# Splitting every other prompt weight with rounding and accumulating transfers issued from POOL, one conditioning part per sequence, and trigonometric tables stored in two parts

## The chip, the cores and the metric

The kernel runs on one core of one Trainium2 chip. The metric is the device time of one execution in microseconds (us), the median of several runs. Engines are named as in the profile: PE (matrix multiplications; PEld are its weight loads), DVE (vector), ACT (activations and copies), POOL (small scalar work before the change), SP (issues the DMAs).

## The reference

One layer of an encoder is applied to two sequences that share all weights: a prompt of 512 rows ("p") and a sample of 1024 rows ("s"), each 1024 wide, in float32.

```
h = rms_norm(x, g_pre_mix) * (1 + sc1) + sh1          # sh, sc, gt from silu(c) @ w_ada, six parts
xa, ya, xb, ga, gb = split(h @ w_in)
xa = depthwise_conv(xa)                                # 4 taps
h_lru = rg_lru(xa, forward) + rg_lru(xa, backward)     # two gates by head, then a scan over time
y_a = (h_lru * gelu(ya)) @ w_a_out
y_b = real(fft2(xb by group)) @ w_b_out
x = x + gt1 * rms_norm((sigmoid(ga) * y_a + sigmoid(gb) * y_b) @ w_o, g_post_mix)
h = rms_norm(x, g_pre_ffn) * (1 + sc2) + sh2
val, gate = split(depthwise_conv(h @ w_up))            # 3 taps
x = x + gt2 * rms_norm((gelu(gate) * val) @ w_down, g_post_ffn)
```

The conditioning vector c differs by sequence, so each of the six parts (shift, scale and gate, for two sub-layers) is needed once for p and once for s. The gates gt1 and gt2 are the third part of each.

## The kernel before, in words

**Products in three passes.** A float32 operand is held as a rounded high part and a remainder (hi, lo), and a product is the sum of three matmuls: hi by hi, hi by lo, lo by hi. For a weight the order inside each block of 128 rows is w.hi with x.hi, w.hi with x.lo, w.lo with x.hi (`passes`, L206, `fm_mm`, L209), so the lo part of a weight is first wanted at the third matmul of its unit.

**Units.** A weight tile of 128x1024 (512 KB) is a unit. `load_unit` (L122) has SP fetch it into one of three `raw` buffers; `prep_unit` (L126) splits it into one of four `hl` buffers: the high part is a copy on ACT (L109, where `on_act` is set) or on DVE (L111), the low part a subtraction on DVE (L112). A prompt unit is 24 matmuls of 512 columns.

**Order.** `emit` (L170) walks a list of steps written by hand. Before the matmuls of unit i it prepares the unit i+3 and issues loads up to three units beyond that; a unit's `hl` buffer is the one that the fourth unit before it leaves. All engines run their instructions in the order of the program, and so does SP with its DMA issues: one that waits for a free `raw` buffer holds up those behind it. `defer` puts the second half of an operation some steps later.

**The prompt's mixer.** After a lead-in come, in this order: projections (ga, xa, gb, two units to a group, f = 0 and f = 1) with four RG-LRU units woven in (`lru_step`, L666), the forward transform of the folded Fourier input (`pq_steps`, L821, whose inputs are fetched back from DRAM as `hr` and paired up on DVE and ACT), four groups of the gelu gate (`ya_steps`, L769), two units of trigonometric tables (`dft_steps`, L884), and `merge_steps` (L936): four groups g, each of two units of w_a (24 matmuls each) and two short units of w_b (13 matmuls of 258 columns each, prepared on DVE alone). For g = 0 the w_a units come first, for the others the w_b units. Into the merge the rows of the sample's first norm are woven: for each of 8 tiles a square with its sum on ACT (L413), two instructions on POOL (L430, L431), and one step later the scaling on ACT (L418).

**An RG-LRU unit** has 24 matmuls into four PSUM buffers. ACT follows with eight tanh (L684), four exp (L692), four tanh (L694) and two relu (L696) in the same step, and one step later, behind a table load, two square roots (L710). DVE multiplies, scans and adds (L703 to L723).

**Conditioning.** `ada_steps(2)` computes the gate part gt1 with eight weight tiles from DRAM and, for each of them, a product with a running sum on DVE for p and one for s (L337): 16 steps placed among the prompt's ya units. `gate_rows` (L363) transposes the result and stores it to DRAM, from where `gate_steps` (L372) broadcasts the rows.

**The sample's mixer** repeats this with one unit to a group and 48 matmuls to a projection unit. Feed-forward parts follow.

Of the kernel before, what the change touches and what calls it, by code (L numbers as in the profile page):

```python
# [18 lines left out]
KT = D // 128  # L19
# [42 lines left out]
class Unit:  # L62
    def __init__(self, src, cols, mix=False, on_act=False, whole=True):
        self.src, self.cols, self.mix, self.on_act, self.whole = src, cols, mix, on_act, whole
        self.raw = self.hi = self.lo = None
# [7 lines left out]
class Enc:  # L73
# [47 lines left out]

    def load_unit(self, u):  # L122
        u.raw = self.sb.tile([128, u.cols], F32, tag="raw", bufs=RAW_BUFS, name=self.nm("raw"))
        self.nc.sync.dma_start(out=u.raw, in_=u.src)

    def prep_unit(self, u):  # L126
        hl = self.sb.tile([128, 2, u.cols], F32R, tag="hl", bufs=HL_BUFS, name=self.nm("hl"))
        u.hi, u.lo = hl[:, 0, :], hl[:, 1, :]
        src = u.raw
        if u.mix:  # L130
            nc = self.nc
            src = self.big([128, u.cols], name="wb")
# [20 lines left out]
    def load_to(self, k):  # L153
        while self.ld < min(len(self.units), k):
            if self.units[self.ld].unit is not None:
                self.load_unit(self.units[self.ld].unit)
            self.ld += 1

    def prep_to(self, k):
        while self.pp < min(len(self.units), k):  # L160
            self.load_to(self.pp + 1)
            u = self.units[self.pp]
            if u.pre is not None:
                u.pre()
# [67 lines left out]

    def fm_steps(self, sq, table, tiles, xh, xl, post, on_act=False):
        box = {}
        steps = []
        for f, m in enumerate(tiles):
            u = Unit(table[m], KT * 128, on_act=on_act)

# [82 lines left out]

    def ada_steps(self, job):

# [9 lines left out]
        def dot(k, s):  # L333
            def f():
                w = box.pop(k) if s else box[k]
                out = w if s else self.big([128, 1024], name="adap")
                nc.vector.scalar_tensor_tensor(  # L337
                    out=out, in0=w, scalar=0.5, in1=self.cvec[s], op0=ALU.mult, op1=ALU.mult,
                    accum_out=self.mod[:, job, s, k:k + 1])
            return f  # L340

        def out():
            bias = self.vec[:, V_BADA + job * 8:V_BADA + job * 8 + 8]
            sub, kind = divmod(job, 3)
            for s in range(2):
                m = self.mod[:, job, s, :]
                nc.vector.tensor_tensor(out=m, in0=m, in1=bias, op=ALU.add)
            for s in range(2):
                m = self.mod[:, job, s, :]
# [4 lines left out]
                if kind == 2:  # L354
                    g = self.vec[:, (V_GOM, V_GOF)[sub]:(V_GOM, V_GOF)[sub] + 8]
                    nc.vector.tensor_tensor(out=self.gtg[:, sub, s, :], in0=m, in1=g, op=ALU.mult)
        steps = [Step(loads=[] if s else [ld(k)], post=dot(k, s)) for k in range(8) for s in range(2)]
        steps += [Step(post=out)]
        if job % 3 == 2:
            steps += [Step(), Step(), Step(), Step(mm=lambda: self.gate_rows(job // 3))]  # L360
        return steps

    def gate_rows(self, sub):  # L363
        nc = self.nc
        ps = self.ps([16, 128])
        self.trans(ps, self.gtg[:, sub].rearrange("p s k -> p (s k)"), self.ident)
        sb = self.sb.tile([16, 128], F32, tag="gaterow", bufs=1, name=self.nm("gr"))
        nc.vector.tensor_copy(sb, ps)
        self.grow[sub] = self.dram([16, 128], f"grow{sub}")
        self.defer(lambda: nc.sync.dma_start(out=self.grow[sub], in_=sb), 1)  # L370

    def gate_steps(self, sq, sub, box):  # L372
        def ld():
            box["gate"] = self.big([128, 1024], name="gate")
            src = self.grow[sub].rearrange("(s k) c -> s (k c)", s=2)[sq.idx:sq.idx + 1, :]
            self.nc.sync.dma_start(out=box["gate"], in_=src.to_broadcast([128, 1024]))
# [289 lines left out]
    def lru_step(self, sq, g, box, hs):  # L666
        nc = self.nc
        n, nf = sq.n, sq.nf
        cols = nf * 512
        u = Unit(self.a["w_lru_" + sq.name][g], cols)  # L670
        th = {}
# [69 lines left out]
    def mix_heads(self, sq, hb, hs, sig, lead=0):  # L741
# [6 lines left out]
        def proj(nm, g, post):  # L748
            return self.fm_steps(sq, self.a[nm], tiles(g), xh, xl, post, on_act=True)

# [18 lines left out]
    def ya_steps(self, sq, hb, hs, yb):  # L769
# [15 lines left out]
        for g in range(sq.groups):  # L785
            tiles = range(g * sq.nf, (g + 1) * sq.nf)
            steps += self.fm_steps(sq, self.a["w_ya"], tiles, lambda: hb["hi"], lambda: hb["lo"],
                                   lambda ps, g=g: post(ps, g), on_act=True)
        steps[-1].post, last = None, steps[-1].post
# [94 lines left out]
    def dft_steps(self, sq, pq, z):  # L884
# [51 lines left out]
    def merge_steps(self, sq, yb, z, sig, mg):  # L936
# [5 lines left out]
        for g in range(sq.groups):  # L942
# [62 lines left out]
            for f in range(nf):  # L1005
# [3 lines left out]
            as_ = self.fm_steps(sq, self.a["w_a"], range(g * nf, (g + 1) * nf),  # L1009
                                lambda: yb["hi"], lambda: yb["lo"], post_a, on_act=True)  # L1010
            first, second = (as_, bs) if g == 0 else (bs, as_)
# [392 lines left out]
def encoder(ctx: ExitStack, tc: tile.TileContext, a, outs):  # L1404
# [6 lines left out]
    with tc.manual_schedule():  # L1411
# [24 lines left out]
        steps = place(steps, side, [ya - 10] + [ya - 4 + i for i in range(16)] + [ya + 13] + [ya + 22] * 9)  # L1436
# [26 lines left out]
def _dft(n):  # L1463
# [6 lines left out]
    for fn in (np.cos, np.sin):  # L1470
# [4 lines left out]
        w = (w * (0.5 / math.sqrt(n))).reshape(rows // 128, 128, nch, HALF).transpose(2, 1, 0, 3)  # L1475
        out.append(np.ascontiguousarray(w.astype(np.float32)).reshape(nch, 128, rows // 128 * HALF))
    return out


# [90 lines left out]
```

## Time and profile before

| | |
|---|---|
| median of 3 runs | 2103.14 us (2102.98 to 2104.68) |
| the profiled execution's own time | 2103.23 us |
| its span, first to last instruction | 2101.1 us |
| around the span | 2.1 us |
| busy in the span: PE, PEld, DVE, ACT, POOL | 98%, 80%, 68%, 45%, 3% |
| granted TensorE clock, mean | 0.997 of full speed |
| DMA traffic | 284.57 MB, all issued by SP |

Busy time of PE says little by itself, since matmuls are pipelined and a matmul that waits for the next weight still counts. The idle time of PEld, the weight loads, shows where PE had to wait for an operand.

### The profile page before, as it was taken

To read this page: it belongs to the slowest core of one execution; us is meant where nothing else is said; L and a number is where in the kernel's file an instruction comes from. 1 tells how busy PE (TensorE), PEld (TensorE's weight loads), DVE (VectorE), ACT (ScalarE), POOL (GpSimd) and SP (SyncE) were. 2 spreads that over 40 slices of the span, in tenths; PEclk is the share of its full clock that TensorE was granted. 3 is DMA by queue.
4 is the path that set the end of the run, shared out by engine and by line. 5 is a ranking of instruction groups with operands and counts; after the bars stand their busy time and mean duration, and the time that the engine had idled before them with its cause. 6 is when DMAs were issued, how large, how long until landed. Compare 5 with 4: busy or idle time off the path is not lost.

```text
span 2101.1 us, 24339 instructions
## 1 busy us (share of the span) xinstructions
PE 2068.3 (98%) x9602; PEld 1687.5 (80%) x9602; DVE 1420.8 (68%) x1798; ACT 944.8 (45%) x1213; POOL 55.3 (3%) x132
## 2 busy tenths in 40 slices
PE   7999999999999999999999999999999999999998
PEld 6777778888888888888888888888888888888887
DVE  4677888677667664656576445749687887875553
ACT  2377555355565632135333336633344444454442
POOL 0000010000000000000100001000000000000000
PEclk9999999999999999999999999999999999999999
DMA  9643475632233314343543324332122222284422
GB/s 342 206 131 130 145 259 188 236 135 96 100 105 99 112 50 145 121 146 122 217 147 116 111 96 166 100 123 88 61 76 83 83 81 81 100 313 165 143 92 109
DMA packets 91121, 284.57 MB, mean 135 GB/s; under 512 B 9056, under 2 KB 20736, under 8 KB 91008
## 3 DMA queue, kind: packets, MB, share of 16 engines
q1 hardware_dynamic: 91008, 283.03, 39.3%
q8 instruction: 75, 1.23, 0.2%
q14 instruction: 38, 0.31, 0.0%
HBM read 237.87 MB, written 45.12 MB: 135 GB/s over the span
## 4 chain that ended last, share of the span: by engine, by line
PE 87%; DVE 5%; ACT 4%; issue 2%; DMA 2%; POOL 0%; SPq 0%; DVEq 0%; POOLq 0%; ACTq 0%
PE ps L201 86%; PE ps L204 1%; DVE hl L112 1%; ACT th L684 1%; ACT th L694 1%; DVE xc L658 1%; ACT ea L692 1%; DMA hr<-hrowp 1%; ACT xn L413 0%; DVE th L715 0%; DVE th L720 0%; DVE th L718 0%; DMA x<-in_x_sample_dram 0%; DMA x<-in_x_prompt_dram 0%; ACT hl L109 0%
## 5 line engine op out<-in xcount | busy, mean ns | idle before, releaser
L201 PE MATMUL ps<-hh,hl 128*128 128x512 f32 x2144 | 632.6, 394 | 3.5 <-DVE hl L112 3.0
L201 PEld LDWEIGHTS ps<-hh,hl 128*128 128x128 f32 x2144 | 402.2, 188 | 99.5 <-DVE hl L112 4.3
L201 PE MATMUL ps<-hl,ah 128*128 128x512 f32 x1440 | 452.3, 395 | 0.0
L112 DVE TENSOR_TENSOR hl<-raw,hl 128x1024 fp32r<-128x1024 f32 (+2 forms) x240 | 286.8, 1200 | 172.3 <-ACT hl L109 170.8
L201 PE MATMUL ps<-hl,hl 128*128 128x512 f32 x1072 | 380.8, 394 | 0.0
L201 PE MATMUL ps<-hx,wq 128*128 128x512 f32 x1596 | 370.9, 394 | 0.0
L109 ACT ACTIVATE hl<-raw 128x1024 fp32r<-128x1024 f32 (+1 forms) x222 | 232.5, 1053 | 279.3 <-PE ps L201 235.2
L201 PEld LDWEIGHTS ps<-hx,wq 128*128 128x128 f32 x1596 | 299.7, 188 | 71.0 <-DVE wq L1251 0.2
L201 PEld LDWEIGHTS ps<-hl,ah 128*128 128x128 f32 x1440 | 269.0, 188 | 61.8
L201 PE MATMUL ps<-hl,al 128*128 128x512 f32 x720 | 283.9, 394 | 0.0
L201 PEld LDWEIGHTS ps<-hl,hl 128*128 128x128 f32 x1072 | 201.4, 188 | 47.6
L201 PEld LDWEIGHTS ps<-hl,al 128*128 128x128 f32 x720 | 135.2, 188 | 32.0
L1347 DVE SCALAR_TENSOR_TENSOR cf<-ps,vec,cf 128x511 f32<-128x511 f32 (+1 forms) x100 | 75.3, 808 | 83.7 <-ACT cf L1339 83.5
L201 PE MATMUL ps<-yh,hl 128*128 128x512 f32 x384 | 111.8, 394 | 0.6 <-DVE yb L991 0.3
L1250 ACT ACTIVATE wq<-wsum 128x512 fp32r<-128x512 f32 x76 | 46.1, 629 | 118.0 <-DVE wsum L1261 118.0
L1195 DVE SCALAR_TENSOR_TENSOR cf<-cq,vec,cf 128x1023 f32<-128x1023 f32 x76 | 97.1, 1277 | 0.0
L1339 ACT ACTIVATE cf<-ps,vec 128x512 f32<-128x512 f32 (+1 forms) x50 | 39.1, 827 | 105.8 <-PE ps L201 105.8
L201 PEld LDWEIGHTS ps<-yh,hl 128*128 128x128 f32 x384 | 71.5, 188 | 17.6 <-DVE yb L991 0.8
L112 DVE TENSOR_TENSOR al<-fq,ah 128x512 fp32r<-128x512 f32 x88 | 57.2, 686 | 32.3 <-PE ps L201 18.4
L201 PE MATMUL ps<-hx,hl 128*128 128x512 f32 x288 | 66.9, 394 | 0.0
L201 PE MATMUL ps<-yl,hl 128*128 128x512 f32 x192 | 65.3, 394 | 0.0
L658 DVE SCALAR_TENSOR_TENSOR xc<-ps,vec,xc 128x511 f32<-128x511 f32 (+3 forms) x48 | 46.9, 1012 | 25.7 <-ACT xc L650 25.1
(182 smaller groups left out, 2325.0 us busy)
## 6 DMA issues: line engine op xcount, KB each, us to landing
raw<-in_w_up_dram SPq DMA_DIRECT2D x88, 512.0 KB, 3.5
raw<-in_w_down_dram SPq DMA_DIRECT2D x66, 512.0 KB, 3.5
ada<-in_w_adaT_dram SPq DMA_DIRECT2D x32, 512.0 KB, 4.9
raw<-in_w_o_dram SPq DMA_DIRECT2D x24, 512.0 KB, 3.5
fs<-cf SPq DMA_DIRECT2D x22, 512.0 KB, 2.6
fq<-fs SPq DMA_DIRECT2D x22, 512.0 KB, 6.0
ada<-in_w_ada_dram SPq DMA_DIRECT2D x16, 512.0 KB, 8.5
raw<-in_w_gb_dram SPq DMA_DIRECT2D x16, 512.0 KB, 4.3
```

The lines of the kernel that those rows point to most:

```text
L109: nc.scalar.activation(out=hi, in_=src, func=AF.Copy)
L112: nc.vector.tensor_tensor(out=lo, in0=src[:, 0:keep], in1=hi[:, 0:keep].bitcast(F32), op=ALU.subtract)
L201: self.nc.tensor.matmul(*args, **kw)
L204: self.nc.tensor.transpose(*args)
L658: nc.vector.scalar_tensor_tensor(out=xc[:, f, o], in0=ps[:, f, o.start + d:o.stop + d], scalar=w[:, tap:tap + 1], in1=xc[:, f, o], op0=ALU ...
L684: nc.scalar.activation(out=t[:, f, :], in_=ps[:, f, :], func=AF.Tanh, scale=0.5, bias=self.halfb[:, b:b + 1])
L692: nc.scalar.activation(out=ea[:, f, :], in_=r[:, f, :], func=AF.Exp, scale=self.nk4[:, k:k + 1], bias=self.nk4[:, k:k + 1])
L694: nc.scalar.activation(out=r[:, f, :], in_=r[:, f, :], func=AF.Tanh, scale=self.k2[:, k:k + 1], bias=self.k2[:, k:k + 1])
L1195: nc.vector.scalar_tensor_tensor(out=box[key][:, o], in0=c[:, i], scalar=self.vec[:, V_FW + 3 * m + t:V_FW + 3 * m + t + 1], in1=box[key][ ...
L1250: nc.scalar.activation(out=hi, in_=src, func=AF.Copy)
L1339: nc.scalar.activation(out=acc[:, f, :], in_=ps[:, f, :], func=AF.Identity, scale=w[:, 1:2], bias=self.vec[:, V_FB + m:V_FB + m + 1])
L1347: nc.vector.scalar_tensor_tensor(out=acc[:, f, o], in0=ps[:, f, o.start + d:o.stop + d], scalar=w[:, tap:tap + 1], in1=acc[:, f, o], op0=A ...
```

## The change

1. In the prompt (and only there) the second unit of each pair (f = 1) of the projections, of ya and of w_a is split by transfers issued from POOL: `load_unit` fetches the weight from DRAM with rounding straight into the hi half of an `hl` buffer; `prep_unit` has ACT write minus hi into the lo half, and POOL issues a second transfer of the same weight from DRAM that adds into lo. The subtraction on DVE and the `raw` buffer go.
2. Such a unit is loaded only when it is the next to be prepared, and prepared no earlier than two units before its matmuls (`load_to`, `prep_to`).
3. The tables of `dft_steps`, for both sequences, lie in DRAM as two rounded parts; POOL's transfer fetches both into the `hl` buffer, and nothing is prepared.
4. The high part of the RG-LRU weights, for both sequences, is a copy on ACT and not on DVE.
5. `ada_steps(2)` is done for p among the prompt's ya units (8 products in place of 16) and for s in the sample's mixer, where the eight weight tiles are fetched again; `gate_rows` and `gate_steps` go by sequence.

```diff
     def load_unit(self, u):
+        if u.parts or u.dma:
+            hl = self.sb.tile([128, 2, u.cols], F32R, tag="hl", bufs=HL_BUFS, name=self.nm("hl"))
+            u.hi, u.lo = hl[:, 0, :], hl[:, 1, :]
+            self.nc.gpsimd.dma_start(out=hl if u.parts else u.hi, in_=u.src)
+            return
...
     def prep_unit(self, u):
+        if u.parts:
+            return
+        if u.dma:
+            self.nc.scalar.activation(out=u.lo, in_=u.hi.bitcast(F32), func=AF.Copy, scale=-1.0)
+            self.nc.gpsimd.dma_start(out=u.lo, in_=u.src, accum_op=ALU.add)
+            return
...
     def load_to(self, k):
         while self.ld < min(len(self.units), k):
+            u = self.units[self.ld].unit
+            if u is not None and (u.parts or u.dma) and self.ld > self.pp:
+                return
...
     def prep_to(self, k):
             u = self.units[self.pp]
+            if u.unit is not None and (u.unit.parts or u.unit.dma) and self.pp + 2 > k:
+                break
...
-    def fm_steps(self, sq, table, tiles, xh, xl, post, on_act=False):
+    def fm_steps(self, sq, table, tiles, xh, xl, post, on_act=False, by_dma=False):
...
-            u = Unit(table[m], KT * 128, on_act=on_act)
+            u = Unit(table[m], KT * 128, on_act=on_act, dma=by_dma and f == 1)
...
-        u = Unit(self.a["w_lru_" + sq.name][g], cols)
+        u = Unit(self.a["w_lru_" + sq.name][g], cols, on_act=True)
...
-            return self.fm_steps(sq, self.a[nm], tiles(g), xh, xl, post, on_act=True)
+            return self.fm_steps(sq, self.a[nm], tiles(g), xh, xl, post, on_act=True, by_dma=sq.nf == 2)
...
-                u = Unit(self.a[f"{name}_{sq.name}"][c], nk * HALF)
+                u = Unit(self.a[f"{name}_{sq.name}"][c], nk * HALF, parts=True)
...
-        steps = [Step(loads=[] if s else [ld(k)], post=dot(k, s)) for k in range(8) for s in range(2)]
+        steps = [Step(loads=[ld(k)] if s == seqs[0] else [], post=dot(k, s)) for k in range(8) for s in seqs]
...
-        side = [e.cond_step()] + e.ada_steps(2) + [Step(), Step()] + e.gate_steps(p, 0, gate["p", 0])
+        side = [e.cond_step()] + e.ada_steps(2, (0,)) + [Step(), Step()] + e.gate_steps(p, 0, gate["p", 0])
...
-        steps += place(mix(s, heads), e.ada_steps(3) + e.ada_steps(4), [0, *range(8, 37), *range(36, 46)])
+        steps += place(mix(s, heads), e.ada_steps(3) + e.ada_steps(4) + e.ada_steps(2, (1,)),
+                       [0, *range(8, 37), *range(36, 46), *range(40, 48)])
```

The calls for ya and w_a get the same `by_dma=sq.nf == 2` (nf is 2 for the prompt, 1 for the sample).

## Rows read from the trace of the kernel before

**Rows 1.** Busy time by stretch: span, then busy us and instructions by engine, clock, DMA

```profile
62.00:323.00 261.00, 247.10 (x1158) 200.24 (x1157) 204.66 (x260) 157.16 (x193) 9.48 (x16) 0.99 0.51 173
...
600.00:800.00 200.00, 200.00 (x864) 161.78 (x862) 128.13 (x129) 100.16 (x93) 0.00 (x0) 1.00 0.27 89
```

**Rows 2.** Waits of PEld, 62 to 113 us: us in total, times, longest

```profile
PEld ps L201 <- ACT eh L109: 2.3, 2, 1.5
PEld ps L201 <- DVE el L112: 1.9, 2, 1.0
```

**Rows 3.** Waits of PEld, 113 to 268 us

```profile
PEld ps L201 <- DVE hl L112: 6.2, 5, 2.3
PEld ps L201 <- DVE hl L111: 1.9, 2, 1.6
PEld ps L201 <- issue: 1.9, 1, 1.9
PEld ps L201 <- ACT th L684: 0.9, 1, 0.9
```

**Rows 4.** Waits of PEld, 268 to 324 us

```profile
PEld ps L201 <- DVE mg L1000: 2.1, 1, 2.1
PEld ps L201 <- DVE hl L112: 1.8, 4, 0.7
PEld ps L201 <- DVE hl L111: 1.2, 2, 0.7
PEld ps L201 <- DVE yb L991: 0.8, 1, 0.8
```

**Rows 5.** Waits of PEld, 324 to 2095 us

```profile
PEld ps L201 <- DVE wq L1251: 0.2, 1, 0.2
```

**Rows 6.** Groups of instructions, 62 to 323 us: busy us, mean ns, idle before

```profile
L112 DVE TENSOR_TENSOR hl<-raw,hl 128x1024 fp32r<-128x1024 f32 x36 | 43.3, 1221 | 11.0 <-ACT hl L109 10.9
L337 DVE SCALAR_TENSOR_TENSOR ada<-ada,cs 128x1024 f32<-128x1024 f32 x8 | 9.8, 1220 | 0.1
...
L418 ACT ACTIVATE xn<-x,sm 128x1024 f32<-128x1024 f32 x8 | 9.2, 1153 | 10.1 <-POOL sm L431 10.1
L413 ACT ACTIVATE xn<-x 128x1024 f32<-128x1024 f32 x8 | 8.4, 1050 | 10.2 <-DMA x<-in_x_sample_dram 10.2
L430 POOL TENSOR_SCALAR sm<-sm 128x1 f32<-128x1 f32 x8 | 4.6, 578 | 286.0 <-ACT xn L413 286.0
```

**Rows 7.** Waits of SP's queue, 62 to 336 us

```profile
SPq L124 <- DVE hl L112: 194.8, 44, 13.6
```

**Rows 8.** Timeline of ACT about the third RG-LRU unit: start, duration

```profile
187.00 4.98 ACT L684 ACTIVATE th<-ps,halfb 128x512 f32<-128x512 f32 x8
...
200.29 1.04 ACT L109 ACTIVATE hl<-raw 128x1024 fp32r<-128x1024 f32 x1
...
202.64 2.01 ACT L710 ACTIVATE th<-th 128x1024 f32<-128x1024 f32 x2
```

**Rows 9.** Timeline of PEld, first load of that unit and of the next

```profile
184.70 0.19 PEld L201 LDWEIGHTS ps<-xch,hl 128*128 128x128 f32 x1
...
190.28 0.19 PEld L201 LDWEIGHTS ps<-hh,hl 128*128 128x128 f32 x1
```

**Rows 10.** Timeline of PEld, two w_b units and the unit behind them

```profile
306.10 0.90 PEld L201 LDWEIGHTS ps<-z,hl 128*128 128x128 f32 x6
...
309.36 0.19 PEld L201 LDWEIGHTS ps<-yh,hl 128*128 128x128 f32 x1
```

**Rows 11.** DMA issues of the page: count, KB, median us to landing

```profile
ada<-in_w_ada_dram SPq DMA_DIRECT2D x16, 512.0 KB, 8.5
...
raw<-in_w_ga_dram SPq DMA_DIRECT2D x14, 512.0 KB, 3.5
raw<-in_w_xa_dram SPq DMA_DIRECT2D x12, 512.0 KB, 4.4
...
raw<-in_w_lru_s_dram SPq DMA_DIRECT2D x8, 256.0 KB, 2.8
```

More of the change, by code (lines that the diff above doesn't have):

```diff
@@ L62, with __init__ @@
 class Unit:
-    def __init__(self, src, cols, mix=False, on_act=False, whole=True):
+    def __init__(self, src, cols, mix=False, on_act=False, whole=True, parts=False, dma=False):
+        self.parts, self.dma = parts, dma
         self.src, self.cols, self.mix, self.on_act, self.whole = src, cols, mix, on_act, whole
@@ L320, in cond_step, with ada_steps @@
         return Step(loads=[ld], post=post)
-    def ada_steps(self, job):
+    def ada_steps(self, job, seqs=(0, 1)):
         nc = self.nc
@@ L334, in f @@
             def f():
-                w = box.pop(k) if s else box[k]
-                out = w if s else self.big([128, 1024], name="adap")
+                end = s == seqs[-1]
+                w = box.pop(k) if end else box[k]
+                out = w if end else self.big([128, 1024], name="adap")
                 nc.vector.scalar_tensor_tensor(
@@ L344, in out @@
             sub, kind = divmod(job, 3)
-            for s in range(2):
+            for s in seqs:
                 m = self.mod[:, job, s, :]
                 nc.vector.tensor_tensor(out=m, in0=m, in1=bias, op=ALU.add)
-            for s in range(2):
+            for s in seqs:
                 m = self.mod[:, job, s, :]
@@ L356, in out, with gate_rows, store @@
                     nc.vector.tensor_tensor(out=self.gtg[:, sub, s, :], in0=m, in1=g, op=ALU.mult)
-        steps = [Step(loads=[] if s else [ld(k)], post=dot(k, s)) for k in range(8) for s in range(2)]
+        steps = [Step(loads=[ld(k)] if s == seqs[0] else [], post=dot(k, s)) for k in range(8) for s in seqs]
         steps += [Step(post=out)]
         if job % 3 == 2:
-            steps += [Step(), Step(), Step(), Step(mm=lambda: self.gate_rows(job // 3))]
+            steps += [Step(), Step(), Step(), Step(mm=lambda: self.gate_rows(job // 3, seqs))]
         return steps
-    def gate_rows(self, sub):
+    def gate_rows(self, sub, seqs):
         nc = self.nc
-        ps = self.ps([16, 128])
-        self.trans(ps, self.gtg[:, sub].rearrange("p s k -> p (s k)"), self.ident)
-        sb = self.sb.tile([16, 128], F32, tag="gaterow", bufs=1, name=self.nm("gr"))
+        r = 8 * len(seqs)
+        ps = self.ps([r, 128])
+        self.trans(ps, self.gtg[:, sub, seqs[0]:seqs[-1] + 1].rearrange("p s k -> p (s k)"), self.ident)
+        sb = self.sb.tile([r, 128], F32, tag="gaterow", bufs=1, name=self.nm("gr"))
         nc.vector.tensor_copy(sb, ps)
-        self.grow[sub] = self.dram([16, 128], f"grow{sub}")
-        self.defer(lambda: nc.sync.dma_start(out=self.grow[sub], in_=sb), 1)
+        for i, s in enumerate(seqs):
+            self.grow[sub, s] = self.dram([8, 128], f"grow{sub}{s}")
+        def store():
+            for i, s in enumerate(seqs):
+                nc.sync.dma_start(out=self.grow[sub, s], in_=sb[8 * i:8 * i + 8, :])
+        self.defer(store, 1)
     def gate_steps(self, sq, sub, box):
@@ L374, in ld @@
             box["gate"] = self.big([128, 1024], name="gate")
-            src = self.grow[sub].rearrange("(s k) c -> s (k c)", s=2)[sq.idx:sq.idx + 1, :]
+            src = self.grow[sub, sq.idx].rearrange("(o k) c -> o (k c)", o=1)
             self.nc.sync.dma_start(out=box["gate"], in_=src.to_broadcast([128, 1024]))
@@ L787, in ya_steps @@
             steps += self.fm_steps(sq, self.a["w_ya"], tiles, lambda: hb["hi"], lambda: hb["lo"],
-                                   lambda ps, g=g: post(ps, g), on_act=True)
+                                   lambda ps, g=g: post(ps, g), on_act=True, by_dma=sq.nf == 2)
         steps[-1].post, last = None, steps[-1].post
@@ L1009, in merge_steps @@
             as_ = self.fm_steps(sq, self.a["w_a"], range(g * nf, (g + 1) * nf),
-                                lambda: yb["hi"], lambda: yb["lo"], post_a, on_act=True)
+                                lambda: yb["hi"], lambda: yb["lo"], post_a, on_act=True,
+                                by_dma=sq.nf == 2)
             first, second = (as_, bs) if g == 0 else (bs, as_)
@@ L1435, in encoder @@
         steps += weave(e.merge_steps(p, yb["p"], z["p"], sig["p"], mg["p"]), sa, 1, 1)
-        steps = place(steps, side, [ya - 10] + [ya - 4 + i for i in range(16)] + [ya + 13] + [ya + 22] * 9)
+        steps = place(steps, side, [ya - 10] + [ya - 4 + i for i in range(8)] + [ya + 6] + [ya + 22] * 9)
         steps += weave(e.rows_steps(p, a["w_o"], mg["p"], gate["p", 0], a["x_prompt"], x2["p"]), sbt, 0, 1)
         _, heads = e.mix_heads(s, h1["s"], hs["s"], sig["s"])
-        steps += place(mix(s, heads), e.ada_steps(3) + e.ada_steps(4), [0, *range(8, 37), *range(36, 46)])
+        steps += place(mix(s, heads), e.ada_steps(3) + e.ada_steps(4) + e.ada_steps(2, (1,)),
+                       [0, *range(8, 37), *range(36, 46), *range(40, 48)])
         pa, pbt = e.h_steps(p, x2["p"], 1, h2["p"])
@@ L1475, in _dft, with _short @@
         w = (w * (0.5 / math.sqrt(n))).reshape(rows // 128, 128, nch, HALF).transpose(2, 1, 0, 3)
-        out.append(np.ascontiguousarray(w.astype(np.float32)).reshape(nch, 128, rows // 128 * HALF))
-    return out
+        w = w.reshape(nch, 128, rows // 128 * HALF)
+        hi = _short(w)
+        out.append(np.ascontiguousarray(np.stack([hi, _short(w - hi)], 2).astype(np.float32)))
+    return out
+def _short(w):
+    m, e = np.frexp(w)
+    return np.ldexp(np.rint(m * 4096.0), e - 12)
 def _fold():
```

## The prediction

> **What bounds the kernel now.** I read the busy times by stretch first. From 600 to 800 us PE does 864 matmuls in 200 us [rows 1], 0.2315 us each, at a granted clock of 1.00: this is its pace when nothing is late. From 62 to 323 us, the prompt's mixer, no engine but PE is near full (DVE 204.7 of 261 us, ACT 157.2), and PE's own busy time hides its waits. So the second view is the waits of PEld. Behind 324 us they come to 0.2 us [rows 5]: there PE sets the time, and nothing taken from DVE, ACT or SP can be gained. Ahead of that they are 4.2 us in the forward transform [rows 2], 10.9 us in the projections, RG-LRU units and ya [rows 3], and 5.9 us in the merge [rows 4]: 21.0 us, 1% of the span, is all that this change can win. Nearly all of these waits are for DVE, a subtraction above all. Third, SP's queue: it waited 194.8 us for subtractions to free a raw buffer [rows 7].
>
> **The gain.** 17 units of the prompt (9 in the projections, 4 in ya, 4 in w_a) lose their subtraction, 17 x 1.22 = 20.7 us of DVE [rows 6]; eight conditioning products lose 8 x 1.22 = 9.8 us; the RG-LRU casts and the two tables some 5 us more. That is 35 of 204.7 us of DVE in this stretch, and fewer raw buffers are asked for, so that SP reaches the fetches of hr earlier, which are what the transform's pairing waits for. I take all 21.0 us as gone. That is the far end: below it nothing can be gained, and where a wait stays the sum is that much worse.
>
> **The price.** A split unit now needs a chain: the rounding transfer when its buffer comes free, the negation on ACT (1.04 us, by the copy of the same size [rows 8]), the adding transfer, then PE at the third matmul of the unit. Call A the time from the end of the negation to the landing of the adding transfer, POOL's work included. No row shows a transfer issued by POOL or one that adds. Lower bound: the quietest plain 512 KB load from SP, 3.5 us [rows 11]. Upper bound: the slowest group of 512 KB loads, 8.5 us [rows 11]. The nearest are the loads of this stage, 4.4 us; the adding transfer moves its destination through the engines as well, and the second 256 KB of a load cost 3.5 - 2.8 = 0.7 us [rows 11], so 512 KB more cost 1.4: 5.8. For POOL writing out the transfer I round up to A = 6.0.
>
> The Trainium skill gives another price ("DMA: Bandwidth & Descriptors", section on the anatomy of a DMA on the SWDGE path): about 2.0 us plus the bytes over 436 GB/s, which for 512 KB is an estimate of 3.2 us. By it the sum below would be -13 us, 2090 us in all. The rows of plain loads, 3.5 to 4.4 us, lie above it already, and no row here shows a transfer from POOL.
>
> *Behind an RG-LRU unit.* By the order of the steps, four split units (the second of gb1, xa3, gb3 and ya1) are negated only two steps after the RG-LRU unit whose buffer they get, behind all of its work on ACT. In the third RG-LRU unit PE moved on at 190.28 [rows 9] and the square roots ended at 202.64 + 2.01 = 204.65 [rows 8], 14.4 us later. A copy of 1.04 us in that stretch goes (the one at 200.29), but the negation of an earlier split unit comes in ahead of the tanh, so 14.4 stays and the negation ends 15.4 us behind the RG-LRU unit. PE wants the result after three units and two matmuls: 3 x 24 x 0.2315 + 0.46 = 17.2 us. PE waits A - 1.8 each: 4 x 4.2 = 16.8 us. Before, the copy stood ahead of the roots and DVE finished the split in time. Queued behind the late negation on ACT are the next unit's copy and conv_a's or gelu's eviction; on POOL the next rounding transfer. Both have slack of a unit or more.
>
> *In the merge.* Here the short w_b units leave little time. The second w_a unit of groups 1 and 2 gets the buffer of a w_b or w_a unit; then come two w_b units (309.36 - 306.10 = 3.26 us [rows 10]), one w_a unit (5.56) and two matmuls: 9.3 us. POOL's queue now holds a rounding transfer that waits for this buffer, and behind it stand the two small instructions of a row tile, for which ACT waits: 1.3 (10.1 us over 8 [rows 6]), scaling 1.15, square 1.05 with 0.2 to read its sum, again 1.3 and 1.15, then the negation 1.05: 7.2 us. PE waits A - 2.1 each: 7.8 us for two. In group 3 no row tiles are left: transfer 4.4 + negation 1.05 + A - 9.3 = 2.15. In group 0 the tables (36 matmuls at 3.26/26 = 0.125, 4.5 us) and one w_a unit pass, 10.5 us with two matmuls, and the negation ends at about 6.0 behind the copies of the tables' result: A - 4.5 = 1.5. Together 11.45.
>
> *At nothing.* The other nine split units (two in the lead-in) have 11 to 17 us for a chain of 8 to 13. The sample's half of the conditioning adds 10 us of DVE and eight loads where DVE is busy 128 of 200 us [rows 1] and PE waits 0.2 us in all [rows 5]; if DVE were full there it would cost those 10. The RG-LRU copies on ACT (1.04 each in the prompt, half in the sample) stand ahead of their units by three steps. The tables' transfers are issued three units ahead.
>
> **The sum.** -21.0 + 16.8 + 11.45 = +7.25 us. The profiled execution took 2103.23 us, 2.1 around its span of 2101.1, and the median of the runs is 2103.14, the same within its spread. Forecast 2103.2 + 7.3 = 2110.5 us, slower. Each microsecond of A is worth 8 us (eight units wait in turn), and the sum is zero at A = 5.1. What a measurement of this kernel can tell from no change is about 0.2%, 4.2 us: A from 4.6 to 5.6.
>
> **Rivals.**
>
> *The adding transfer is as quick as a plain load (faster).* At A = 4.4 the four units behind RG-LRU wait 2.6 each (10.4), the merge 4.6 + 0.55, and the sum is -5.4: 2098 us; at 3.5 it is 6.8 + 2.8 - 21.0 = -11.4: 2092. It decides below A = 4.6. For it: 16 DMA engines were busy only 51% in this stretch [rows 1], so a second pass over SBUF might be hidden inside the fetch. The Trainium skill's fit, named above, gives less still. Against it: the plain loads of this stage already take 4.4, and here POOL has to write the transfer out first. 0.30.
>
> *The waits only change hands (same).* DVE is relieved, but PE then waits for the adding transfers as long as it waited for subtractions: A between 4.6 and 5.6, 2099 to 2107 us. The page would show the same PEld idle time under another releaser. 0.22.
>
> *POOL's queue is the new bound (much slower).* All 36 new transfers go in order through one queue that before did 16 small instructions in this stretch; if writing out one takes POOL so long that A reaches the 8.5 us of the slowest loads, the sum is -21.0 + 26.8 + 12.8 + 4.65 + 4.0 = +27: 2130 us. Nothing in the trace shows such a queue. 0.08, part of the slow side.
>
> **How the numbers follow.** The forecast is A about 5.6 to 7.5 with a chance of 0.40 (2107 to 2122; at 7.0 the sum is -21.0 + 20.8 + 9.8 + 3.15 + 2.5 = +15), the last rival takes 0.08. Slower by over 0.2%: 0.48; within: 0.22; faster: 0.30. The range for 8 in 10 runs from 2093 (A near 3.6) to 2122: it leaves out the quickest transfers and the rival of a clogged POOL. The forecast's own range is 2107 to 2122.
>
> **What the profile after would show.** PEld's waits in the transform gone, with SP's waits on subtractions well under 195 us. PEld idle before the loads of eight units, released by a DMA into hl, some 4 us each behind RG-LRU and 1.5 to 4 us in the merge. In the ACT timeline, the negation behind the square roots. The rounding transfer near 4.4 us and the adding one near 5 to 6 from issue to landing. Waits behind the merge still near zero. The prediction is wrong if the negations come ahead of the roots, if A is below 4.6, or if new waits show up in the sample's mixer, where I cost everything at nothing.

## The result, and the profile after

The changed kernel took 2129.77 us (median of four runs, 2128.57 to 2133.94), the kernel before 2103.06 us in the same comparison: a ratio of 1.013, 95% interval 1.0112 to 1.0147. It is 26.7 us slower, where 7.3 were forecast, and lies outside the range. The profiled execution took 2130.4 us with a span of 2128.6, 27.5 us more than before.

Busy time by stretch, the columns of [rows 1]:

```profile
62.00:323.00 261.00, 237.54 (x1078) 192.88 (x1077) 164.57 (x203) 154.56 (x189) 29.62 (x44) 0.95 0.64 192
600.00:800.00 200.00, 200.00 (x864) 161.97 (x863) 135.67 (x133) 117.69 (x111) 0.00 (x0) 1.00 0.30 99
```

DVE was indeed relieved, from 204.7 to 164.6 us. PE nevertheless lost 9.6 us of busy time in this stretch, and two numbers at the end of the row moved that the prediction didn't use: the granted clock fell from 0.99 to 0.95, the DMA share rose from 0.51 to 0.64. Behind 600 us PE runs as before.

The waits of PEld follow: from 113 to 268 us (three lines), from 268 to 350 us (one), and behind 350 us (three); total, count, longest, without the lines of 0.2 us. From 62 to 113 us there are none, against 4.2 us [rows 2].

```profile
PEld ps L218 <- DMA hl<-in_w_gb_dram: 7.4, 2, 4.1
PEld ps L218 <- DMA hl<-in_w_ya_dram: 4.7, 2, 3.5
PEld ps L218 <- DMA hl<-in_w_xa_dram: 4.3, 2, 3.8
...
PEld ps L218 <- DMA hl<-in_w_a_dram: 17.1, 3, 6.5
...
PEld ps L218 <- DMA hl<-in_w_a_dram: 2.2, 1, 2.2
PEld ps L221 <- ACT z L119: 0.9, 1, 0.9
PEld ps L218 <- DVE z L121: 0.6, 1, 0.6
```

The subtractions of [rows 3, 4] are gone as a cause; in their place stand transfers into `hl`. One by one, in the timeline of PEld (start, duration, in brackets the idle time before), these are the eight units that the prediction named:

```profile
134.78 0.50 PEld L218 LDWEIGHTS ps<-hh,hl 128*128 128x128 f32 x2 [3.27 <-DMA hl<-in_w_gb_dram]
167.56 0.30 PEld L218 LDWEIGHTS ps<-hh,hl 128*128 128x128 f32 x2 [3.81 <-DMA hl<-in_w_xa_dram]
212.02 0.30 PEld L218 LDWEIGHTS ps<-hh,hl 128*128 128x128 f32 x2 [4.08 <-DMA hl<-in_w_gb_dram]
245.86 0.30 PEld L218 LDWEIGHTS ps<-hh,hl 128*128 128x128 f32 x2 [3.51 <-DMA hl<-in_w_ya_dram]
290.55 0.50 PEld L218 LDWEIGHTS ps<-yh,hl 128*128 128x128 f32 x2 [5.20 <-DMA hl<-in_w_a_dram]
315.24 0.50 PEld L218 LDWEIGHTS ps<-yh,hl 128*128 128x128 f32 x2 [5.32 <-DMA hl<-in_w_a_dram]
337.42 0.50 PEld L218 LDWEIGHTS ps<-yh,hl 128*128 128x128 f32 x2 [6.55 <-DMA hl<-in_w_a_dram]
356.03 0.30 PEld L218 LDWEIGHTS ps<-yh,hl 128*128 128x128 f32 x2 [2.19 <-DMA hl<-in_w_a_dram]
```

How such a wait comes about is seen about the third RG-LRU unit, in the timelines of ACT and POOL; it answers to [rows 8]:

```profile
202.94 2.01 ACT L734 ACTIVATE th<-th 128x1024 f32<-128x1024 f32 x2
204.85 1.05 ACT L136 ACTIVATE hl<-hl 128x1024 fp32r<-128x1024 f32 x1
...
206.33 0.86 POOL L137 DMA_DIRECT2D hl<-in_w_gb_dram  x1 [14.27 <-ACT hl L136]
```

The negation stands right behind the square roots and ends at 205.90, POOL starts to write out the adding transfer at 206.33, and PE goes on at 212.02: the length A of the prediction is 6.1 us here.

What the waits don't show is the clock. Stretches of 5 us across the first and the fifth of these gaps and behind them:

```profile
130.00:135.00 5.00, 2.16 (x10) 1.46 (x9) 4.93 (x5) 3.52 (x4) 0.88 (x2) 0.92 0.78 165
135.00:140.00 5.00, 5.00 (x17) 3.99 (x18) 5.00 (x8) 0.00 (x0) 0.00 (x0) 0.73 0.43 150
...
290.00:295.00 5.00, 4.45 (x11) 3.54 (x12) 0.00 (x0) 0.00 (x0) 0.00 (x0) 0.53 1.03 419
```

Once the weight is there PE is busy throughout from 135 to 140 us, but it gets through 17 matmuls, not the 21.6 that 5 us hold at the pace of [rows 1] (864 in 200 us); from 290 to 295 us the granted clock is near the lower of its two levels, 1.2 of 2.4 GHz. The same is seen behind each of the seven gaps of 3.27 us and more; behind the last, of 2.19 us, the clock stays at 1.00.

**An account.** For each kernel I added up, in its profiled execution, the waits of PEld behind 62 us and, over stretches of 5 us from 60 to 400 us, PE's busy time times (1 - granted clock). What is left of the span differs by 0.7 us between the kernels before and changed, so these two terms are nearly their whole difference; over all runs the rest lies between 2077.8 and 2082.4 us (e4 apart), so a few microseconds stay open in some of them. The medians are over all runs of a kernel (in e12 the profiled execution was the slowest of five); the kernel before has 2103.06 to 2103.89 us in the five comparisons.

| kernel | median us | span | waits | clock | rest |
|---|---|---|---|---|---|
| before | 2103.1 | 2101.1 | 21.3 | 1.5 | 2078.3 |
| changed | 2129.8 | 2128.6 | 37.8 | 11.8 | 2079.0 |
| e1, no adding transfers | 2095.9 | 2094.4 | 16.4 | 0.0 | 2078.0 |
| e2, adding transfers alone | 2127.3 | 2126.5 | 36.7 | 12.0 | 2077.8 |
| e3, nine units | 2097.1 | 2095.4 | 13.4 | 2.5 | 2079.5 |
| e4, filler | 2122.8 | 2120.5 | 9.3 | 0.0 | 2111.2 |
| e5, six units | 2092.7 | 2090.9 | 11.1 | 0.0 | 2079.8 |
| e6, negation on POOL | 2125.3 | 2122.3 | 33.4 | 8.7 | 2080.2 |
| e7, row tiles behind the merge | 2147.3 | 2146.0 | 54.2 | 12.6 | 2079.2 |
| e8, w_a plain | 2107.5 | 2106.8 | 18.8 | 7.3 | 2080.7 |
| e12, as e6, w_a plain | 2096.5 | 2098.5 | 11.8 | 4.3 | 2082.4 |
| e9, tables alone | 2103.2 | 2101.9 | 20.6 | 2.9 | 2078.4 |
| e10, conditioning alone | 2108.4 | 2106.5 | 23.3 | 3.0 | 2080.2 |
| e11, RG-LRU copies alone | 2101.6 | 2100.9 | 17.6 | 4.9 | 2078.4 |
| e13, conditioning and tables | 2099.4 | 2097.0 | 17.2 | 1.6 | 2078.2 |

In e4 29.9 us of added matmuls stand in the rest (129 x 0.2315), so it is 2081.3 there. In e10 another 2.7 us of clock lie behind 400 us, from 825 to 835 us. The change costs 16.5 us of waits and 10.3 us of clock, 26.8 of the 27.5 us.

### The profile page after: what moved, and what is told of

The parts are those of the page before. It is cut to its first block, busy times and chain, and to the rows that moved or that the text cites. A ratio compares the mean times of both kernels' runs of the same rounds, so it can differ in the third digit from the quotient of the medians.

```text
span 2128.6 us, 24376 instructions
## 1 busy us (share of the span) xinstructions
PE 2077.4 (98%) x9603; PEld 1695.0 (80%) x9603; DVE 1387.8 (65%) x1758; ACT 951.6 (45%) x1225; POOL 83.9 (4%) x172
## 3 DMA queue, kind: packets, MB, share of 16 engines
q8 instruction: 75, 1.23, 0.2%
## 4 chain that ended last, share of the span: by engine, by line
PE 91%; DMA 3%; issue 3%; DVE 1%; ACT 1%; POOL 0%; SPq 0%; DVEq 0%; POOLq 0%; ACTq 0%
PE ps L218 90%; DMA hl<-in_w_a_dram 2%; PE ps L221 1%; DMA hl<-in_w_gb_dram 1%; DVE ada L355 0%; DMA wxbt<-in_wxbT_dram 0%; DMA hl<-in_w_ya_dram 0%; DMA hl<-in_w_xa_dram 0%; ACT hl L136 0%; ACT xn L437 0%; DVE yl L113 0%; DVE gl L801 0%; POOL hl L127 0%; ACT yh L110 0%; POOL sm L455 0%
## 5 line engine op out<-in xcount | busy, mean ns | idle before, releaser
L113 DVE TENSOR_TENSOR hl<-raw,hl 128x1024 fp32r<-128x1024 f32 (+2 forms) x217 | 260.4, 1203 | 185.7 <-ACT hl L110 185.2
L110 ACT ACTIVATE hl<-raw 128x1024 fp32r<-128x1024 f32 (+2 forms) x217 | 223.8, 1037 | 263.5 <-PE ps L218 245.7
L218 PE MATMUL ps<-yh,hl 128*128 128x512 f32 x384 | 116.8, 408 | 17.5 <-DMA hl<-in_w_a_dram 17.5
L218 PEld LDWEIGHTS ps<-yh,hl 128*128 128x128 f32 x384 | 74.1, 196 | 36.0 <-DMA hl<-in_w_a_dram 19.3
L761 ACT ACTIVATE sg<-ps 128x1024 f32<-128x1024 f32 x24 | 24.6, 1026 | 94.9 <-PE ps L218 83.5
```

What stands on the lines that cost most here:

```text
L110: nc.scalar.activation(out=hi, in_=src, func=AF.Copy)
L113: nc.vector.tensor_tensor(out=lo, in0=src[:, 0:keep], in1=hi[:, 0:keep].bitcast(F32), op=ALU.subtract)
L218: self.nc.tensor.matmul(*args, **kw)
L761: self.nc.scalar.activation(out=t, in_=ps, func=AF.Tanh, scale=0.5)
```

## The experiments

**e1: the weights split on chip again, all else as changed.**

```diff
-            u = Unit(table[m], KT * 128, on_act=on_act, dma=by_dma and f == 1)
+            u = Unit(table[m], KT * 128, on_act=on_act, dma=False)
```

> The changed kernel with its 17 prompt units split on chip again (ACT copy, DVE subtraction); the RG-LRU copies on ACT, the sample's conditioning beside the sample's mixer and the tables in two parts stay. Theory: the +27 us of the change are the late chain of rounding transfer, negation and adding transfer at eight units (34 us of PEld waits) and the granted clock that falls behind each of those gaps (about 13 us of PE at less than full speed between 60 and 345 us). Without the chains both go, some waits for subtractions come back: 2097 to 2103 us. Rival: the cost lies in the other edits (tables by POOL, conditioning moved, RG-LRU copies on ACT): 2115 us or more.

2095.89 us, ratio 0.9962 (0.9947 to 0.9977), a little below the theory's range and faster than the kernel before. The waits of before are only partly gone (16.4 of 21.3 us are left), but the clock never falls. The whole loss belongs to the 17 units that are split by transfers (edits 1 and 2).

**e2: the same transfers alone on the kernel before.** The lines for `dma` in `load_unit`, `prep_unit`, `load_to` and `prep_to` (edits 1 and 2) come with it, none of the other edits does.

```diff
-            u = Unit(table[m], KT * 128, on_act=on_act)
+            u = Unit(table[m], KT * 128, on_act=on_act, dma=by_dma and f == 1)
```

> The kernel before with the split by rounding and adding transfers alone; RG-LRU copies on DVE, tables split on chip, conditioning of both sequences in the prompt, as before. Theory (late chains and the clock behind their gaps): the same eight waits of 2 to 7 us and the same fall of the clock, with some waits for subtractions on top of them: 2125 to 2135 us. Rival (the other edits cost the time): near 2103 us.

2127.28 us, ratio 1.0109 (1.0093 to 1.0126). The theory's number; the waits are those of the changed kernel within 1.1 us in each stretch, and the "waits for subtractions on top" that I expected aren't there.

**e3: adding transfers only for the nine units that were in time.**

```diff
-            return self.fm_steps(sq, self.a[nm], tiles(g), xh, xl, post, on_act=True, by_dma=sq.nf == 2)
+            return self.fm_steps(sq, self.a[nm], tiles(g), xh, xl, post, on_act=True,
+                                 by_dma=sq.nf == 2 and (nm, g) not in (("w_gb", 1), ("w_xa", 3), ("w_gb", 3)))
...
-                                   lambda ps, g=g: post(ps, g), on_act=True, by_dma=sq.nf == 2)
+                                   lambda ps, g=g: post(ps, g), on_act=True, by_dma=sq.nf == 2 and g != 1)
```

(and no `by_dma` for w_a)

> The changed kernel with rounding and adding transfers only for the nine prompt units whose chain was in time (gb01, ga11, xa21, ga21, gb21, ga31, ya01, ya21, ya31); the eight that came late are split on chip. Theory: a chain that is in time costs nothing, so the eight waits and the loss of clock go, and DVE keeps the relief of nine subtractions: 2085 to 2097 us, faster than the kernel before. Rival: transfers by POOL and the second fetch of each unit cost time wherever they stand (other transfers late, more waits elsewhere): 2115 us or more.

2097.07 us, ratio 0.9968 (0.9955 to 0.9981), at the edge of the theory's range; the rival falls. But one chain was late that had been in time before. The timeline from 237 to 246 us, all engines:

```profile
237.42 1.06 ACT L110 ACTIVATE yh<-gl 128x1024 fp32r<-128x1024 f32 x1 [7.60 <-DVE gl L802]
238.39 1.04 ACT L136 ACTIVATE hl<-hl 128x1024 fp32r<-128x1024 f32 x1
...
239.86 0.87 POOL L137 DMA_DIRECT2D hl<-in_w_ya_dram  x1 [15.24 <-DVE yl L113]
...
245.29 0.50 PEld L218 LDWEIGHTS ps<-hh,hl 128*128 128x128 f32 x2 [4.72 <-DMA hl<-in_w_ya_dram]
```

The negation of ya21's weight is queued behind a copy on ACT that waited 7.60 us for gelu's product on DVE. A chain through ACT's queue is late whenever anything ahead of it is.

**e4: matmuls that nobody needs, put into the gaps.** The unit's first product is repeated into a bank that the real one overwrites; work is added and nothing left out.

```diff
+                for _ in range(pad if f == 1 else 0):
+                    self.mmul(box["ps"][:, f, 0:512], lhsT=u.hi[:, 0:128], rhs=xh()[0][:, 0:512], start=True, stop=True)
```

> The changed kernel with matmuls added that nobody needs, in front of the third matmul of the eight late units (14 each behind the RG-LRU units, 20, 20, 24 and 9 in the merge), which repeat the unit's first product on the rounded half into a bank that the first real product overwrites: 129 matmuls, some 30 us of PE work put into gaps of about 34 us. Theory (part of the loss is the granted clock that falls behind each gap): PE runs on through the gaps, the clock stays at 1.00, and the kernel gets about 8 to 13 us faster than the changed one although it does more: 2117 to 2122 us. Rival (the clock plays no part, the time is lost in the waits alone): 2130 us or more.

2122.77 us, ratio to the kernel before 1.009 (1.0075 to 1.0105), just above the theory's range: 7 us below the changed kernel with 129 matmuls more. The stretches of the gaps shown above:

```profile
130.00:135.00 5.00, 5.00 (x23) 4.04 (x22) 4.97 (x5) 4.45 (x5) 1.43 (x2) 1.00 0.61 106
135.00:140.00 5.00, 5.00 (x23) 4.07 (x22) 4.97 (x7) 0.00 (x0) 0.00 (x0) 1.00 0.58 171
```

The clock stays at 1.00 throughout, and 135 to 140 us holds 23 matmuls in place of 17. The waits were filled (37.8 to 9.3 us) by work of 29.9 us, which by itself gains nothing; the time came from the clock.

**e5: six units only**, e3 with ya split on chip too.

```diff
-                                   lambda ps, g=g: post(ps, g), on_act=True, by_dma=sq.nf == 2 and g != 1)
+                                   lambda ps, g=g: post(ps, g), on_act=True)
```

> The changed kernel with rounding and adding transfers only for six units of the projections (gb01, ga11, xa21, ga21, gb21, ga31); ya and w_a are split on chip. The run with nine such units kept one late chain, a wait of 4.72 us in ya whose negation stood behind a copy on ACT that waited for gelu's product. Theory (time is lost only where a chain is late, and the clock falls behind that gap): without it the 4.7 us and the loss of clock behind it go, some 2 us of waits for subtractions come back: 2090 to 2094 us. Rival (transfers by POOL cost in themselves, and the one late wait was hidden in nothing): as the run with nine or slower, 2097 us or more.

2092.65 us, ratio 0.9949 (0.9936 to 0.9961): within the theory's range and the fastest kernel found, 11 us ahead of the kernel before. Its waits from 113 to 268 us:

```profile
PEld ps L218 <- DVE hl L113: 4.8, 5, 2.2
PEld ps L218 <- ACT th L708: 3.0, 2, 1.9
```

Every adding transfer that is left is in time (0.3 us of waits in the lead-in), and the six cost nothing. Of the 11 us they bring some 3: the other edits alone, in e1, gave 2095.89 us.

**e6: the negation on POOL**, in the queue in which both transfers stand.

```diff
-            self.nc.scalar.activation(out=u.lo, in_=u.hi.bitcast(F32), func=AF.Copy, scale=-1.0)
+            self.nc.gpsimd.tensor_scalar(out=u.lo, in0=u.hi.bitcast(F32), scalar1=-1.0, scalar2=None, op0=ALU.mult)
```

> The changed kernel with the negation on POOL instead of ACT, so that rounding transfer, negation and adding transfer of a unit stand in one queue and nothing of ACT is in the chain. Theory A (behind the RG-LRU units the chain is late because the negation stands behind tanh, exponentials and square roots on ACT): the four waits of 3.3 to 4.1 us there go, with the clock that fell behind them; a negation takes 1 to 2 us on POOL, so the chain from the buffer's release is about 5 + 2 + 5.5 = 12.5 us and the room 17.2. In the merge the room is 9.3 us, so waits of 2 to 4 us stay there, and row tiles stand behind the negation in POOL's queue: 2105 to 2118 us in all. Theory B (the transfers themselves take the 17 us): waits of 3 to 4 us stay behind the RG-LRU units too, 2125 us or more.

2125.33 us, ratio 1.0105 (1.0089 to 1.012): the total points at theory B, the place of the waits at A. Waits of PEld from 113 to 268 us, then from 268 to 350 us, and POOL's negations from 62 to 360 us as a group:

```profile
PEld ps L218 <- DMA hl<-in_w_ya_dram: 3.4, 2, 2.9
PEld ps L218 <- DMA hl<-in_w_ga_dram: 1.3, 1, 1.3
PEld ps L218 <- DMA hl<-in_w_xa_dram: 1.0, 1, 1.0
...
PEld ps L218 <- DMA hl<-in_w_a_dram: 25.4, 4, 10.2
...
L136 POOL TENSOR_SCALAR hl<-hl 128x1024 fp32r<-128x1024 f32 x15 | 43.9, 2925 | 70.4 <-DMA hl<-in_w_ya_dram 27.4 <-DMA hl<-in_w_gb_dram 17.7 <-DMA hl<-in_w_a_dram 10.3
```

Behind the RG-LRU units the four waits of 3.3 to 4.1 us are gone but for 0.5 in ya1: the order on ACT made them, not the transfers. The wait of 2.9 us is another unit's, the second of ya0, which waited 1.23 in the changed kernel. I had the merge too low: a negation takes 2.93 us on POOL against 1.05 on ACT, the row tiles' small instructions share its queue, and the four w_a waits grow from 19.3 to 25.4 us.

**e7: the sample's row tiles behind the merge.**

```diff
-        steps += weave(e.merge_steps(p, yb["p"], z["p"], sig["p"], mg["p"]), sa, 1, 1)
+        steps += e.merge_steps(p, yb["p"], z["p"], sig["p"], mg["p"]) + sa
```

The last tile is transposed for the first group ahead of its scaling there, so the sample's output isn't the reference's.

> The changed kernel with the sample's eight row tiles (loads, squares, scalings, their small instructions on POOL) behind the prompt's merge instead of between its steps. To be read from the four waits before the second w_a units (5.20, 5.32, 6.55 and 2.19 us in the changed kernel), not from the total, because the row tiles lose their cover and may hold up the steps behind the merge by up to 15 us: 2105 to 2135 us. Theory A (the first three are longer than the fourth because the row tiles stand before the negation on ACT, and their loads share the DMA engines with the adding transfers): the waits of groups 1 and 2 come down to that of group 3, some 2 us, and that of group 0 to 1 to 3. Theory B (they are longer for what lies between release and use on PE, which the row tiles don't touch): they stay at 5 us or more.

2147.33 us, ratio 1.021 (1.0196 to 1.0224), more than my range: the uncovered row tiles make PE wait 19.7 us. The four waits of the merge:

```profile
288.90 0.40 PEld L218 LDWEIGHTS ps<-yh,hl 128*128 128x128 f32 x2 [2.74 <-DMA hl<-in_w_a_dram]
311.31 0.30 PEld L218 LDWEIGHTS ps<-yh,hl 128*128 128x128 f32 x2 [3.59 <-DMA hl<-in_w_a_dram]
328.05 0.30 PEld L218 LDWEIGHTS ps<-yh,hl 128*128 128x128 f32 x2 [2.64 <-DMA hl<-in_w_a_dram]
349.82 0.50 PEld L218 LDWEIGHTS ps<-yh,hl 128*128 128x128 f32 x2 [7.57 <-DMA hl<-in_w_a_dram]
```

The first three fall from 5.20, 5.32 and 6.55 us, as theory A has it for the first and the third; the second falls only to 3.59. The fourth was not expected at all: it rises from 2.19 to 7.57 us, where five of the moved x loads and three of w_o are issued in the same 22 us, and the 16 DMA engines are at 0.97 to 1.04 from 340 to 350 us. From POOL's issue to PE it takes 10.7 us there, against 5.4 to 6.3 in the other three. Traffic beside an adding transfer is the likely cause, but no run varies it alone. How much of groups 0 to 2 is traffic and how much the row tiles' work on ACT and POOL, this run doesn't separate.

**e8: only the second w_a units split on chip.**

```diff
-                                lambda: yb["hi"], lambda: yb["lo"], post_a, on_act=True,
-                                by_dma=sq.nf == 2)
+                                lambda: yb["hi"], lambda: yb["lo"], post_a, on_act=True)
```

> The changed kernel with the second w_a units split on chip; the rounding and adding transfers of the projections and ya stay, with the four late ones behind the RG-LRU units. Theory (waits and the clock behind them add up unit by unit): the merge's 19.3 us of waits go and so does its loss of clock, about 8 us by the windows from 280 to 350 us, and 1 to 2 us of waits for subtractions come back: 2102 to 2106 us, of which 14.7 us of waits and some 6 us of clock are left behind the RG-LRU units. Rival (the waits stand for one another: without those of the merge others grow): 2112 us or more.

2107.54 us, ratio 1.0019 (1.001 to 1.0028), between the two and nearer to the theory. From 268 to 350 us 1.2 us of waits are left and the clock is 1.00; the waits behind the RG-LRU units stay, with 7.3 us of clock (5.5 ahead of 280 us in the changed kernel). They don't stand for one another.

**e12: e6 and e8 together** (both diffs on the changed kernel).

> The changed kernel with the negation on POOL and the second w_a units split on chip; the 13 units of the projections and ya keep their rounding and adding transfers. Against the run with the same 13 units and the negation on ACT (2107.5 us, with waits of 3.70, 3.66, 3.53 and 2.91 us behind the RG-LRU units). Theory (those four were late by the negation's place behind the square roots, and the clock falls behind their gaps): about 10 us of waits and 6 to 9 us of clock go, although the negation takes 2.9 us on POOL against 1.04 on ACT: 2088 to 2093 us, as fast as the run with six units or faster. Rival (the order on ACT is not what costs): 2103 us or more.

2096.51 us, ratio 0.9969 (0.9956 to 0.9981): 11 us faster than e8, less than the 16 to 19 of the theory. Of the four late units only the second of xa3 still waits, 0.66 us, so for their waits the theory holds. But two others wait now: the second of gb2, 3.02 us, which was in time, and the second of ya0, 3.72, which waited 1.39 in e8. The stretches in which their adding transfers run:

```profile
170.00:175.00 5.00, 3.59 (x16) 2.58 (x14) 4.96 (x8) 0.00 (x0) 0.58 (x1) 1.00 0.93 207
...
220.00:225.00 5.00, 2.51 (x11) 1.69 (x10) 2.04 (x3) 4.87 (x7) 0.00 (x0) 0.99 1.04 283
```

Here the DMA engines are full, and from POOL's issue to PE it takes 7.9 and 9.1 us, where seven of the eight late units of the changed kernel took 5.3 to 6.2.

**e9, e10, e11: each of the other three edits alone; e13: two of them.** All four are the changed kernel with `dma=False` as in e1 and these edits undone: for e9 the first and the second, for e10 the first and the third, for e11 the second and the third, for e13 the first.

```diff
-        u = Unit(self.a["w_lru_" + sq.name][g], cols, on_act=True)
+        u = Unit(self.a["w_lru_" + sq.name][g], cols)
...
-        side = [e.cond_step()] + e.ada_steps(2, (0,)) + [Step(), Step()] + e.gate_steps(p, 0, gate["p", 0])
+        side = [e.cond_step()] + e.ada_steps(2) + [Step(), Step()] + e.gate_steps(p, 0, gate["p", 0])
...
-                u = Unit(self.a[f"{name}_{sq.name}"][c], nk * HALF, parts=True)
+                u = Unit(self.a[f"{name}_{sq.name}"][c], nk * HALF)
```

> The kernel before with the tables in two parts alone. The three other edits together won 7.8 us (2103.7 to 2095.9 us) when the 17 units were split on chip. Theory A (what counts is DVE work taken out of the stretch from ya to the merge, and the tables are one of the two edits that do this): some 2 us of the merge's 5.9 us of waits go, 2100 to 2103 us. Theory B (the tables stand where PE has slack, so nothing is won): 2103 to 2105 us.

> The kernel before with the third conditioning part split by sequence alone. Theory A (its eight products, 9.8 us of DVE, are what made the merge wait for subtractions): most of the 5.9 us in the merge and the fall of the clock at 290 to 300 us go, 2096 to 2100 us. Theory B (the products lie beside other work in the prompt and cost as much in the sample): 2102 to 2105 us.

> The kernel before with the copies of the RG-LRU units on ACT alone. Theory A (DVE is short in the projections, ACT is not): 2 to 4 us of the 10.9 us of waits from 113 to 268 us go, 2099 to 2102 us. Theory B (ACT is as short there, and its longer queue holds up PE's evictions): 2103 to 2107 us.

> The kernel before with two of the edits together: conditioning by sequence and tables in two parts; RG-LRU copies on DVE, all weights split on chip. Alone they gave 2108.4 and 2103.2 us. Theory A (each needs the other: the conditioning frees the prompt's merge but makes PE wait 8.4 us in the sample's mixer, where its gate rows are transposed while DVE and ACT still split tables; the tables in two parts take that work away): the wait of 8.4 us falls to about 1, the merge's waits stay near 1, 2096 to 2100 us. Rival B (the two merely add up): 2106 to 2109 us.

The tables alone: 2103.17 us, ratio 0.9999 (0.999 to 1.0008), nothing. The RG-LRU copies: 2101.56, ratio 0.999 (0.9981 to 1.0), some 2 us, 4 at most by the interval, as theory A has it; the waits from 113 to 268 us fall from 10.9 to 8.0. The conditioning: 2108.36, ratio 1.0026 (1.0016 to 1.0036), slower than either theory had it. Its waits in the merge do fall from 5.9 to 1.3 us, but in the sample's mixer a new one stands (timelines of PEld, PE and DVE):

```profile
825.12 0.08 PEld L221 LDWEIGHTS ps<-ident,gtg 128*8 128x8 f32 x1 [8.36 <-ACT z L119]
...
825.15 0.37 PE L221 MATMUL ps<-ident,gtg 128*8 128x128 f32 x1 [8.17 <-DVE gtg L374]
...
822.77 0.69 DVE L112 CAST hl<-raw 128x1032 fp32r<-128x1032 f32 x1
823.49 1.23 DVE L113 TENSOR_TENSOR hl<-raw,hl 128x1032 fp32r<-128x1032 f32 x1
824.64 0.16 DVE L365 TENSOR_TENSOR mod<-mod,vec 128x8 f32<-128x8 f32 x1
824.84 0.17 DVE L374 TENSOR_TENSOR gtg<-mod,vec 128x8 f32<-128x8 f32 x1
```

This is the transposition of the sample's gate rows (`gtg`), a PE step that the conditioning brings into the sample's mixer. The profile puts the wait of its weight load down to a copy on ACT, but that had ended at 824.55; DVE ends `gtg` at 825.01, 0.11 us ahead of the load, and in e13 the load follows it by the same 0.11 us. DVE comes to `gtg` only behind this split of a table unit (128x1032), and late already from the work ahead of it, an earlier table's split among it. With the tables in two parts (e13) the wait is 0.9 us and the time 2099.38, ratio 0.9979 (0.997 to 0.9989): rival B of e13, mere addition, falls. Together with the RG-LRU copies the two win 7.8 us (e1); alone the three give -0.4, +4.8 and -2.1.

## Why the prediction was wrong

**What bounds the kernel** was read rightly: what the runs change lies in the waits of PEld ahead of 400 us and the clock behind them, but for the one of e10 at 825 us and its clock.

**The mechanism of the price was right, unit by unit.** The eight units named are the ones that wait 2.19 us or more (no other waits over 1.23), each for its adding transfer, four of them behind a negation that follows the square roots. A was 6.0 in the sum; from the end of the negation to PE it measured 5.7 to 6.6 us at seven of the eight and 8.7 at the first w_a unit (281.85 to 290.55), above the upper bound of 8.5; the trace of before had a slower group of loads than the rows shown (x of the prompt, 9.1). The fit of the Trainium skill ("DMA: Bandwidth & Descriptors", the anatomy of a DMA on the SWDGE path), 3.2 us by the prediction's estimate, doesn't hold for these transfers: no gap gives less than 5.7 us, and even from the end of POOL's writing out to PE it is 4.4 or more.

**The failed step is the sum's rule that each microsecond of waiting is worth one microsecond**, "each microsecond of A is worth 8 us (eight units wait in turn)". It priced the gaps by their length alone. PE comes out of seven of them at a lower granted clock, which cost another 10.3 us over before (11.8 against 1.5). e4 shows it by filling the gaps, e1 and e5 by having no late chain. The rows to suspect it stood in the trace of before, behind the longest wait of [rows 4]:

```profile
289.76 0.78 PEld L201 LDWEIGHTS ps<-z,hl 128*128 128x128 f32 x6 [2.06 <-DVE mg L1000]
...
290.00:295.00 5.00, 4.39 (x20) 3.47 (x19) 4.84 (x13) 3.48 (x6) 1.79 (x2) 0.66 0.91 339
```

None of the three signs of being wrong that the prediction names looks at the clock. The Trainium skill ("TensorE: Matmul & The Clock Gate", section on how oscillation bites in real kernels) describes matmuls that start at 1.2 GHz behind each wait for a DMA and counts half of the throttled time as lost; the trace agrees, with 0.53 granted in the 5 us about the fifth gap's end.

**The term of the merge was mis-sized**: 11.45 us forecast, 19.3 measured (1.5, 3.9, 3.9 and 2.15 against 5.20, 5.32, 6.55 and 2.19). Only group 3, without row tiles, came out as worked out. In group 0 the adding transfer runs beside six loads that SP issues from 282.48 to 287.77 us, with the DMA engines at 0.97 from 285 to 290. In groups 1 and 2 A was right (5.7 and 6.0), but from the issue of the rounding transfer the negation ended after 8.2 and 8.9 us, not 7.2, and PE came to the weight after 8.6 and 8.3, not 9.3; in group 2 the rounding transfer alone took from 322.53 to 330.36, 7.8 us where 4.4 were put down and hidden. The term behind the RG-LRU units, 16.8 us, measured 14.7.

**At nothing** stood the other nine units and the sample: 3.9 us of small waits, 1.23 the longest of the nine units and 0.9 in the sample. That the sample's half of the conditioning is free was right in sum and wrong in reason: what counted was not DVE's spare time but what stands ahead of `gtg` in its order, and e10 waits 8.4 us until the tables are taken off DVE.

**The gain** of 21.0 us came as taken: all of the old waits are gone. But most of it hangs on the units that are late: with none of the 17 by transfers (e1) 16.4 us of waits are left, with the six (e5) 11.1. Whether the other eleven remove the rest by relief of DVE, or because a PE that comes later gives DVE time, no run tells apart.

**The rivals.** Faster and same needed A below 5.6 and fall. "POOL's queue is the new bound" gave 2130 us, the measured number, by another road: POOL is busy 29.6 of 261 us, an adding transfer takes it 0.9 us to issue, and A isn't 8.5 but at one unit.

In terms of the sum: waits +16.5 in place of +7.25, clock +10.3 in place of nothing, together 26.8.

## What to carry to other kernels

Price a gap on PE by its length and the clock behind it: read the granted clock in short stretches across gaps that the trace already has before adding new ones. Moving work from an engine to transfers pays only where the whole chain, from the buffer's release over two transfers and whatever stands ahead on the engine between them, fits into the time before use; choose units by that, one by one (beside the same other edits the kernel was 0.5% faster than before with six of the 17, 0.4% with none and 1.3% slower with all). Edits that relieve the same engine don't add up: test them together as well as alone, for one may open the wait that another closes.

## What the runs showed of the hardware

An adding transfer of 512 KB from POOL took 5.3 to 6.2 us from its issue to PE at seven of the eight late units of the changed kernel, while 99 to 172 GB/s were moved; at four others, with 226 to 312 GB/s, it took 7.9 to 10.7 us (group 0, two in e12, one in e7). Two in e6 don't fit, 5.95 us at 280 GB/s and 7.6 at 197, so traffic alone doesn't settle it. A plain load took 3.5 to 8.5 [rows 11]. A negation of 128x1024 takes 2.93 us on POOL and 1.05 on ACT.

The length of a wait doesn't tell by itself whether the clock falls. Behind the waits of e5, up to 2.19 us, it stayed at 1.00, and behind those of 3.0 us and more in the changed kernel and e12 it fell. But before, it fell to 0.66 behind a wait of 2.06 us (290 to 295 us) and stayed at 1.00 behind one of 2.29 (245 to 250 us); in e9 it fell to 0.66 at that place behind 2.28.
